# Average pooling over 512 MiB on one core: first loads moved ahead of the framework's closing barrier, sums as two additions, scaling on another engine

## The chip, the cores and the metric

The kernel runs on one core of one Trainium2 chip. The metric is the device time of one execution in microseconds (us): the median of several runs, lower is better.

Four of the core's engines appear here. VectorE (DVE in the profile) and ScalarE (ACT) do arithmetic, SyncE (SP) only issues transfers and passes semaphores, and GpSimd (POOL) sets a few constants at the start. Transfers between the chip's memory (HBM) and the on-chip buffer (SBUF, 128 partitions) are carried by 16 DMA engines; SyncE and ScalarE each have a queue through which they feed them.

## The reference

```python
x = randn(64, 256, 8192), float32;  kernel_size = stride = 4
for i in range(out_len):                       # 2048
    output[:, :, i] = np.mean(x[:, :, 4*i : 4*i + 4], axis=2)
```

Each output is the mean of four neighbouring inputs. 536.87 MB are read and 134.22 MB are written.

## The kernel before, in words

The input is taken as one flat array and cut into 64 blocks. A block is 128 partitions by 16,384 float32 (`FULL`), 8 MiB, and gives 128 by 4,096 means. Two input tiles, `xt[0]` and `xt[1]`, hold one block each; two output tiles, `ot[0]` and `ot[1]`, hold the means of two blocks each (a "pair").

The order on each engine is written by hand with semaphores. `take(engine, sem, n)` makes an engine wait until a semaphore is at least `n` and then lowers it by `n`. The framework's Tile context is closed at the start of the function (`tc.close()`, L36 in the profile), and everything after it is placed by hand.

- SyncE issues the loads. The first two go out ahead of the loop; later, `load(i, k)` goes out when VectorE has raised `free`, which says that `xt[k]` has been read. `full[k]` says that a load has landed.
- VectorE waits for `full[k]` (and, at a pair's first block, for `stored[q]`: the output tile's last store has landed). Then one `tensor_reduce` (L76) adds each group of four from `xt[k]` into half of `ot[q]`. After the second block of a pair, `scale` drains VectorE and multiplies the whole output tile by 1/4 (L67), raising `scaled`.
- ScalarE waits for `scaled` and issues the store of the pair (L87), 4 MiB.

`pair(i, q, ahead)` is one such round. The loop has 15 iterations of two pairs; one more pair follows, whose `ahead` issues the last two loads, the very last in three pieces (`TAIL`: 8192, 4608 and 3584 columns, each with a semaphore of its own). Blocks 62 and 63 are then done by `sums` (L92 to L94), which adds in two steps in place:

```python
nc.vector.tensor_tensor(out=t[:, : w // 2], in0=t[:, ::2], in1=t[:, 1::2], op=add)
nc.vector.drain()
nc.vector.tensor_tensor(out=o, in0=t[:, : w // 2 : 2], in1=t[:, 1 : w // 2 : 2], op=add)
```

Each result is scaled on VectorE and stored: block 62 from SyncE's queue (L127), the three pieces of block 63 from ScalarE's (L133).

Of the kernel before, what the change touches and what calls it, by code (L numbers as in the profile page):

```python
# [1 line left out]

# [4 lines left out]

FULL = 16384
PAIR = 2  # L10
ROUND = 2 * PAIR

TAIL = (8192, 4608, 3584)

@with_exitstack
def kernel(
    ctx: ExitStack,
    tc: tile.TileContext,
    x: bass.AP,  # L20
    kernel_size: bass.AP,
    stride: bass.AP,
    out: bass.AP,
):
    nc = tc.nc
    K, S = int(kernel_size), int(stride)
    assert K == S == 4
    B, C, L = x.shape
    assert L % K == 0
    P = nc.NUM_PARTITIONS  # L30
    dt = x.dtype
    add, mult = mybir.AluOpType.add, mybir.AluOpType.mult

    tc.close()
    tc.compile()  # L36

    M = FULL // K
    blocks = B * C * L // P // FULL
    loop = blocks - ROUND  # L40
    assert blocks * P * FULL == B * C * L and blocks % ROUND == 0 and sum(TAIL) == FULL
    xb = x.rearrange("b c l -> (b c l)").rearrange("(n p m) -> n p m", p=P, m=FULL)
    ob = out.rearrange("b c l -> (b c l)").rearrange("(n p m) -> p n m", p=P, m=M)

    xt0 = ctx.enter_context(nc.sbuf_tensor([P, FULL], dt))
    xt1 = ctx.enter_context(nc.sbuf_tensor([P, FULL], dt))
    ot0 = ctx.enter_context(nc.sbuf_tensor([P, PAIR * M], dt))
    ot1 = ctx.enter_context(nc.sbuf_tensor([P, PAIR * M], dt))
    xt, ot = [xt0, xt1], [ot0, ot1]

    full = [nc.alloc_semaphore(f"full{k}") for k in range(2)]
    piece = [nc.alloc_semaphore(f"piece{k}") for k in range(len(TAIL))]
    free = nc.alloc_semaphore("free")
    scaled = nc.alloc_semaphore("scaled")
    scaled_last = nc.alloc_semaphore("scaled_last")
    stored = [nc.alloc_semaphore(f"stored{k}") for k in range(2)]

    def take(engine, sem, n):
        engine.wait_ge(sem, n).then_inc(sem, -n)  # L60

    def load(i, k):
        nc.sync.dma_start(out=xt[k][:, :], in_=xb[i]).then_inc(full[k], 16)

    def scale(o, done):
        nc.vector.drain()  # L66
        means = nc.vector.tensor_scalar(out=o, in0=o, scalar1=1.0 / K, scalar2=None, op0=mult)  # L67
        means.then_inc(done, 1)

    def pair(i, q, ahead):  # L70

        for k in range(PAIR):
            take(nc.vector, full[k], 16)
            if k == 0:
                take(nc.vector, stored[q], 16)
            nc.vector.tensor_reduce(  # L76
                out=ot[q][:, k * M : (k + 1) * M],
                in_=xt[k][:, :].rearrange("p (m k) -> p m k", k=K),
                op=add,
                axis=mybir.AxisListType.X,  # L80
            ).then_inc(free, 1)
            take(nc.sync, free, 1)
            ahead(k)
        scale(ot[q][:, :], scaled)
        take(nc.scalar, scaled, 1)
        o = ot[q][:, :].rearrange("p (n m) -> p n m", n=PAIR)
        nc.scalar.dma_start(out=ob[:, bass.ds(i, PAIR), :], in_=o).then_inc(stored[q], 16)  # L87

    def sums(t, o, loaded):
        w = t.shape[1]  # L90
        take(nc.vector, loaded, 16)
        nc.vector.tensor_tensor(out=t[:, : w // 2], in0=t[:, ::2], in1=t[:, 1::2], op=add)  # L92
        nc.vector.drain()  # L93
        nc.vector.tensor_tensor(  # L94
            out=o, in0=t[:, : w // 2 : 2], in1=t[:, 1 : w // 2 : 2], op=add
        )

    for k in range(2):
        load(k, k)
        nc.scalar.sem_inc(stored[k], 16)  # L100

    edges = [sum(TAIL[:i]) for i in range(len(TAIL) + 1)]
    pieces = list(zip(edges[:-1], edges[1:]))
    xe, oe = xb[blocks - 1], ob[:, blocks - 1, :]

    def ahead_of_last(k):
        if k == 0:
            load(blocks - 2, 0)
        else:
            for sem, (a, b) in zip(piece, pieces):  # L110
                nc.sync.dma_start(out=xt[1][:, a:b], in_=xe[:, a:b]).then_inc(sem, 16)

    engines = (mybir.EngineType.SP, mybir.EngineType.DVE, mybir.EngineType.Activation)
    with nc.Fori(0, loop // ROUND, 1, engines=engines) as r:
        for q in range(2):
            i = r * ROUND + q * PAIR
            pair(i, q, lambda k: load(i + (PAIR + k), k))

    pair(loop, 0, ahead_of_last)

    take(nc.vector, stored[1], 16)
    o = ot[1][:, :M]
    sums(xt[0][:, :], o, full[0])
    scale(o, scaled_last)
    take(nc.sync, scaled_last, 1)
    nc.sync.dma_start(out=ob[:, blocks - 2, :], in_=o).then_inc(stored[1], 16)  # L127
    for sem, (a, b) in zip(piece, pieces):
        o = ot[1][:, M + a // K : M + b // K]
        sums(xt[1][:, a:b], o, sem)  # L130
        scale(o, scaled)
        take(nc.scalar, scaled, 1)
        nc.scalar.dma_start(out=oe[:, a // K : b // K], in_=o).then_inc(stored[1], 16)  # L133
    take(nc.sync, stored[0], 16)
    take(nc.sync, stored[1], 16 * (1 + len(TAIL)))

# [1 line left out]
_INS = ['x', 'kernel_size', 'stride']  # L139
_OUTS = [((64, 256, 2048), 'float32')]  # L140

_NUMBERS = {'kernel_size': 4, 'stride': 4}

# [26 lines left out]
```

## Time and profile before

| what | value |
|---|---|
| time, median of 3 runs | 1556.87 us (1556.68 to 1556.89) |
| the profiled execution: its own time | 1556.91 us |
| the profiled execution: its span | 1555.2 us |
| granted clock | 1.0 |
| VectorE busy | 1236.5 us, 80% of the span |
| ScalarE, TensorE arithmetic | none |
| bytes read and written | 536.87 MB and 134.22 MB, 432 GB/s over the span |

The span runs from the first to the last instruction; the time of the run is 1.7 us longer. The profile counts an engine as busy only while it does arithmetic; instructions that issue transfers, wait or raise semaphores are not counted. A group of instructions is shown by its line in the kernel, its engine, its operation, its tiles and shapes, and the mean duration of one in ns; behind the last bar stands the idle time of the engine ahead of them, and what ended it. In the tables of windows a DMA share of 1.00 means that all 16 DMA engines moved packets all the time; a packet is counted in the window in which it starts, so short windows can show more than 1.

### The profile page before, as it was taken

How to read it: one execution, taken by the hardware profiler on the slowest of the kernel's cores; microseconds unless marked ns; L12 is line 12 of the kernel's file. 1: busy time of each engine (PE TensorE's matmuls, PEld its weight loads, DVE VectorE, ACT ScalarE, POOL GpSimd, SP SyncE). 2: the span in 40 equal slices, each digit the busy share in tenths (PEclk: the TensorE clock that was granted, in tenths of full speed). 3: DMA queues.
4: the chain of work that ended last, by engine and by line, in shares of the span. 5: the costliest groups of instructions: out<-in, count | busy, mean ns of one | idle time of the engine just before them, and what ended most of it. 6: DMA issues, size and time to landing. Idle time of an engine off the chain costs nothing. (4 is left out here: it accounts for less than half of the span.)

```text
span 1555.2 us, 790 instructions
## 1 busy us (share of the span) xinstructions
DVE 1236.5 (80%) x105; POOL 0.2 (0%) x4
## 2 busy tenths in 40 slices
DVE  3968778787797877978779787797877977778778
POOL 0000000000000000000000000000000000000000
DMA  9999999999999999999999999999999999999999
GB/s 405 425 415 447 431 438 432 437 418 433 438 432 438 442 428 424 437 430 442 438 438 432 435 417 436 438 432 438 440 423 431 433 433 443 438 437 433 433 419 404
DMA packets 18512, 671.10 MB, mean 432 GB/s; under 512 B 1616, under 2 KB 1616, under 8 KB 1872
## 3 DMA queue, kind: packets, MB, share of 16 engines
q1 hardware_dynamic: 9648, 538.97, 80.1%
q10 hardware_dynamic: 8864, 132.12, 19.8%
HBM read 536.87 MB, written 134.22 MB: 432 GB/s over the span
## 5 line engine op out<-in xcount | busy, mean ns | idle before, releaser
L76 DVE TENSOR_REDUCE ot<-xt 128x4096 f32<-128x16384 f32 x62 | 1067.6, 17220 | 306.2 <-DVEq L60 306.2
L67 DVE TENSOR_SCALAR ot<-ot 128x8192 f32<-128x8192 f32 (+4 forms) x35 | 142.1, 4061 | 3.2
L92 DVE TENSOR_TENSOR xt<-xt 128x8192 f32<-128x8192 f32 (+3 forms) x4 | 17.7, 4424 | 4.1 <-DVEq L60 4.1
L94 DVE TENSOR_TENSOR ot<-xt 128x4096 f32<-128x4096 f32 (+3 forms) x4 | 9.2, 2292 | 0.3
L152 POOL MEMSET const-bfloat16-1.0<- 128x1 bf16 x1 | 0.1, 101 | 0.0
L152 POOL MEMSET const-uint8-127<- 128x1 uint8 x1 | 0.1, 101 | 0.0
L152 POOL MEMSET const-float32-0.0<- 128x1 f32 x1 | 0.1, 98 | 0.2 <-issue 0.2
L152 POOL MEMSET const-float32-1.0<- 128x1 f32 x1 | 0.1, 98 | 0.0
## 6 DMA issues: line engine op xcount, KB each, us to landing
out_dram<-ot ACTq DMA_DIRECT2D x31, 4096.0 KB, 50.4
xt<-in_x_dram SPq DMA_DIRECT2D x1, 4096.0 KB, 20.7
xt<-in_x_dram SPq DMA_DIRECT2D x1, 2304.0 KB, 31.2
out_dram<-ot SPq DMA_DIRECT2D x1, 2048.0 KB, 18.7
xt<-in_x_dram SPq DMA_DIRECT2D x1, 1792.0 KB, 35.6
out_dram<-ot ACTq DMA_DIRECT2D x1, 1024.0 KB, 11.8
xt<-in_x_dram SPq DMA_DIRECT2D x63, 30.7
out_dram<-ot ACTq DMA_DIRECT2D x1, 576.0 KB, 7.0
```

What stands on the lines that cost most here:

```text
L67: means = nc.vector.tensor_scalar(out=o, in0=o, scalar1=1.0 / K, scalar2=None, op0=mult)
L76: nc.vector.tensor_reduce(out=ot[q][:, k * M : (k + 1) * M], in_=xt[k][:, :].rearrange("p (m k) -> p m k", k=K), op=add, axis=mybir.AxisLi ...
L92: nc.vector.tensor_tensor(out=t[:, : w // 2], in0=t[:, ::2], in1=t[:, 1::2], op=add)
L94: nc.vector.tensor_tensor(out=o, in0=t[:, : w // 2 : 2], in1=t[:, 1 : w // 2 : 2], op=add)
L152: nc = _bacc.Bacc("TRN2", target_bir_lowering=False, num_devices=1)
```

## The change

1. The first two loads are issued ahead of `tc.close()` and `tc.compile()`. `load` returns its instruction, and the two names are put into `tc.no_tile_sem_insts`, so that Tile adds no semaphores of its own to them; they raise `full[0]` and `full[1]` as before.
2. In `pair`, `tensor_reduce` is replaced by `sums`: two additions in place with a drain between them. `sums` no longer waits itself; its callers do.
3. The pair is scaled on ScalarE (`nc.scalar.mul`) and no longer on VectorE. SyncE, which takes `free` after each block, raises the new semaphore `summed` after the second block of a pair and ahead of the load that it then issues; ScalarE takes `summed`, scales, raises `scaled`, takes it, and issues the store.
4. Ahead of the loop ScalarE multiplies a single column of zeros, so that its table (the activation function's data) is loaded there. It raises `stored[0]`.
5. In the tail, block 62 and the first two pieces of block 63 are scaled on ScalarE as well; the last piece (`b == FULL`) is still scaled on VectorE. The semaphore between VectorE and ScalarE is `summed_last`.

```diff
-    tc.close()
-    tc.compile()
...
     def load(i, k):
-        nc.sync.dma_start(out=xt[k][:, :], in_=xb[i]).then_inc(full[k], 16)
+        d = nc.sync.dma_start(out=xt[k][:, :], in_=xb[i])
+        d.then_inc(full[k], 16)
+        return d
...
+    for k in range(2):
+        tc.no_tile_sem_insts.add(load(k, k).ins.name)
+    tc.close()
+    tc.compile()
...
-            nc.vector.tensor_reduce(
-                out=ot[q][:, k * M : (k + 1) * M],
-                in_=xt[k][:, :].rearrange("p (m k) -> p m k", k=K),
-                op=add,
-                axis=mybir.AxisListType.X,
-            ).then_inc(free, 1)
+            sums(xt[k][:, :], ot[q][:, k * M : (k + 1) * M]).then_inc(free, 1)
             take(nc.sync, free, 1)
+            if k == 1:
+                nc.sync.sem_inc(summed, 1)
             ahead(k)
-        scale(ot[q][:, :], scaled)
+        take(nc.scalar, summed, 1)
+        nc.scalar.mul(ot[q][:, :], ot[q][:, :], 1.0 / K).then_inc(scaled, 1)
         take(nc.scalar, scaled, 1)
...
-    for k in range(2):
-        load(k, k)
-        nc.scalar.sem_inc(stored[k], 16)
+    zero = nc.const_aps.tensor(0.0, [P, 1], dt)
+    nc.scalar.mul(ot[0][:, :1], zero, 1.0).then_inc(stored[0], 16)
+    nc.scalar.sem_inc(stored[1], 16)
...
     take(nc.vector, stored[1], 16)
+    take(nc.vector, full[0], 16)
     o = ot[1][:, :M]
-    sums(xt[0][:, :], o, full[0])
-    scale(o, scaled_last)
+    sums(xt[0][:, :], o).then_inc(summed_last, 1)
+    take(nc.scalar, summed_last, 1)
+    nc.scalar.mul(o, o, 1.0 / K).then_inc(scaled_last, 1)
...
-        sums(xt[1][:, a:b], o, sem)
-        scale(o, scaled)
-        take(nc.scalar, scaled, 1)
+        take(nc.vector, sem, 16)
+        last = sums(xt[1][:, a:b], o)
+        if b == FULL:
+            nc.vector.drain()
+            last = nc.vector.tensor_scalar(
+                out=o, in0=o, scalar1=1.0 / K, scalar2=None, op0=mult
+            )
+        last.then_inc(summed_last, 1)
+        take(nc.scalar, summed_last, 1)
+        if b != FULL:
+            nc.scalar.mul(o, o, 1.0 / K).then_inc(scaled, 1)
+            take(nc.scalar, scaled, 1)
```

More of the change, by code (lines that the diff above doesn't have):

```diff
@@ L54 @@
     free = nc.alloc_semaphore("free")
+    summed = nc.alloc_semaphore("summed")
+    summed_last = nc.alloc_semaphore("summed_last")
     scaled = nc.alloc_semaphore("scaled")
@@ L62, in load, with sums @@
     def load(i, k):
-        nc.sync.dma_start(out=xt[k][:, :], in_=xb[i]).then_inc(full[k], 16)
-    def scale(o, done):
+        d = nc.sync.dma_start(out=xt[k][:, :], in_=xb[i])
[5 more added lines that the diff above has]
+    tc.compile()
+    def sums(t, o):
+        w = t.shape[1]
+        nc.vector.tensor_tensor(out=t[:, : w // 2], in0=t[:, ::2], in1=t[:, 1::2], op=add)
         nc.vector.drain()
-        means = nc.vector.tensor_scalar(out=o, in0=o, scalar1=1.0 / K, scalar2=None, op0=mult)
-        means.then_inc(done, 1)
+        return nc.vector.tensor_tensor(
+            out=o, in0=t[:, : w // 2 : 2], in1=t[:, 1 : w // 2 : 2], op=add
+        )
     def pair(i, q, ahead):
@@ L87, in pair @@
         nc.scalar.dma_start(out=ob[:, bass.ds(i, PAIR), :], in_=o).then_inc(stored[q], 16)
[L89 to L96, printed above, removed]
-    for k in range(2):
-        load(k, k)
-        nc.scalar.sem_inc(stored[k], 16)
+    zero = nc.const_aps.tensor(0.0, [P, 1], dt)
+    nc.scalar.mul(ot[0][:, :1], zero, 1.0).then_inc(stored[0], 16)
+    nc.scalar.sem_inc(stored[1], 16)
     edges = [sum(TAIL[:i]) for i in range(len(TAIL) + 1)]
@@ L129 @@
         o = ot[1][:, M + a // K : M + b // K]
-        sums(xt[1][:, a:b], o, sem)
-        scale(o, scaled)
-        take(nc.scalar, scaled, 1)
+        take(nc.vector, sem, 16)
[4 more added lines that the diff above has]
+                out=o, in0=o, scalar1=1.0 / K, scalar2=None, op0=mult
+            )
+        last.then_inc(summed_last, 1)
[3 more added lines that the diff above has]
+            take(nc.scalar, scaled, 1)
         nc.scalar.dma_start(out=oe[:, a // K : b // K], in_=o).then_inc(stored[1], 16)
```

## The prediction

> **What bounds the kernel now.** The page first: which resource has no slack.
>
> ```profile
> span 1555.2 us, 790 instructions
> DVE 1236.5 (80%) x105; POOL 0.2 (0%) x4
> q1 hardware_dynamic: 9648, 538.97, 80.1%
> q10 hardware_dynamic: 8864, 132.12, 19.8%
> ```
>
> VectorE works 80% of the span. The packets of the two DMA queues (q1: SyncE's loads, q10: ScalarE's stores) take 80.1 + 19.8 = 99.9% of all that 16 DMA engines have. The table of windows tells whether that is so everywhere.
>
> ```profile
> 0.00:2.40 2.40, 0.00 (x0) 0.20 (x4) 1.00 0.00 0
> 2.40:21.80 19.40, 0.00 (x0) 0.00 (x0) 1.00 1.03 432
> 21.80:41.20 19.40, 17.22 (x1) 0.00 (x0) 1.00 1.00 432
> 39.20:45.00 5.80, 3.79 (x2) 0.00 (x0) 1.00 0.92 362
> 44.04:48.88 4.84, 4.84 (x1) 0.00 (x0) 1.00 1.00 433
> 189.60:1399.20 1209.60, 972.35 (x76) 0.00 (x0) 1.00 1.00 434
> 1544.40:1550.40 6.00, 5.32 (x5) 0.00 (x0) 1.00 0.98 418
> 1550.40:1553.00 2.60, 0.00 (x0) 0.00 (x0) 1.00 0.97 399
> 1553.00:1555.20 2.20, 0.00 (x0) 0.00 (x0) 1.00 0.09 38
> ```
>
> Columns: window, its length, busy VectorE, busy GpSimd, granted clock, DMA share, GB/s. For 1,209.6 us in the middle the DMA share is 1.00 at 434 GB/s. There are three places where it is not full: the first 2.4 us; a dent near 42 us (5.8 us at 362 GB/s are 2.1 MB, which the row below it moves in 4.84 us: 1.0 us lost); and the last 2.2 us. The bytes are the same in both kernels, so only these places can give time, unless the change opens a new hole or slows the transfers. One round of the loop shows how far the loop is from a hole.
>
> ```profile
> 791.24 17.22 DVE L76 TENSOR_REDUCE ot<-xt 128x4096 f32<-128x16384 f32 x1 [2.66 <-DVEq L60]
> 815.20 17.22 DVE L76 TENSOR_REDUCE ot<-xt 128x4096 f32<-128x16384 f32 x1 [6.74 <-DVEq L60]
> 832.51 4.43 DVE L67 TENSOR_SCALAR ot<-ot 128x8192 f32<-128x8192 f32 x1
> 832.65 0.33 SPq L63 DMA_DIRECT2D xt<-in_x_dram  x1
> 837.18 0.38 ACTq L87 DMA_DIRECT2D out_dram<-ot  x1
> 839.60 17.22 DVE L76 TENSOR_REDUCE ot<-xt 128x4096 f32<-128x16384 f32 x1 [2.66 <-DVEq L60]
> ...
> out_dram<-ot ACTq DMA_DIRECT2D x31, 4096.0 KB, 50.4
> ```
>
> A pair of blocks takes 839.60 - 791.24 = 48.36 us. VectorE idles before each reduction, for data. The load that refills a tile goes out at 832.65, while the other tile's load lands near 839.5: 6.9 us in which the next load already waits behind the running one. The loop stays DMA bound as long as this lead is over the time from a load's issue to its first data: at the start, issue at 1.39 (row below) and nothing before 2.4, so 1.0 us.
>
> **Part 1: VectorE's sums in the loop.** The reduction becomes two additions with a drain, and the scaling leaves VectorE. All shapes stand in the old tail:
>
> ```profile
> L76 DVE TENSOR_REDUCE ot<-xt 128x4096 f32<-128x16384 f32 x62 | 1067.6, 17220 | 306.2 <-DVEq L60 306.2
> L67 DVE TENSOR_SCALAR ot<-ot 128x8192 f32<-128x8192 f32 x31 | 137.2, 4427 | 2.9
> L92 DVE TENSOR_TENSOR xt<-xt 128x8192 f32<-128x8192 f32 x1 | 8.7, 8693 | 2.6 <-DVEq L60 2.6
> L94 DVE TENSOR_TENSOR ot<-xt 128x4096 f32<-128x4096 f32 x1 | 4.4, 4425 | 0.1
> ```
>
> 8.69 + 0.08 + 4.43 = 13.2 us instead of 17.22 per block, 4.0 less; with the scaling gone VectorE has 26.4 us of work per pair, not 38.9. All of it is cover: loads go out 4.0 us earlier, the lead grows from 6.9 to about 10.9 us, and the DMA engines are as full as before. Worth in the loop: 0. If the lead were lost instead, each missing us would be paid 31 times.
>
> **Part 2: scaling on ScalarE.** No ScalarE arithmetic stands in this trace. From below: VectorE's scaling of the same tile, 4.43 us. From above: the reduction, 17.22, the longest single instruction. I take 8.7, the addition that also writes 8,192 elements: it lies between the two, and is the more cautious of the two rows of that size. In the round shown, the sums would end at 815.20 + 13.2 = 828.4 and the store go out at 828.4 + 8.7 + 0.1 = 837.2, where it goes out now (837.18). It must be home before the same output tile is used again at 839.60 + 48.36 = 887.96; it takes 50.4 us, so 837.6 is the latest issue that delays nothing, and ScalarE may take 9.1 us. Later than that VectorE would wait, still without a hole: the sum that frees a tile may start 10.9 - 1.0 = 9.9 us late before the DMA engines run dry. Worth: 0 up to some 19 us of ScalarE time.
>
> The Trainium skill, page "ScalarE: Activation LUTs", section "Rules for kernel authors", speaks against this part: multiplications belong on VectorE, not on ScalarE. The section "What ACT_TABLE_LOAD costs" of the same page prices an activation with immediate scale at 186 ns plus 0.833 ns per element, by which I estimate 7.0 us here; the store would go out at 835.5, the sum would be the same, and VectorE's 4.43 us is indeed less than either.
>
> The table's load stands ahead of the loop on ScalarE, where nothing is queued but the first scaling, due after both first blocks have landed and been summed (42.62 + 13.2 = 55.8 us). Cover: all of that; cost 0. If it ran in front of the first store anyway, that store would still meet a full DMA. On SyncE one semaphore increment is added in front of every second load, a queue step below 0.1 us, covered by the lead.
>
> **Part 3: the first two loads, and the dent.** Rows:
>
> ```profile
> SPq L152 <- PEq L152: 0.5, 1, 0.5
> SPq L36 <- PEq L36: 0.5, 2, 0.3
> ...
> 1.39 0.87 SPq L63 DMA_DIRECT2D xt<-in_x_dram  x2
> ...
> 23.40 17.22 DVE L76 TENSOR_REDUCE ot<-xt 128x4096 f32<-128x16384 f32 x1 [23.40 <-DVEq L60]
> 40.90 19.52 SPq L63 DMA_DIRECT2D xt<-in_x_dram  x2
> 42.62 17.22 DVE L76 TENSOR_REDUCE ot<-xt 128x4096 f32<-128x16384 f32 x1 [2.01 <-DVEq L60]
> ```
>
> SyncE passes the program's opening barrier (L152), then two barriers of the closing Tile context (L36), then issues the loads at 1.39. Now they stand in front of `tc.close()`: the L152 wait stays, the two L36 waits (0.5 us) come after them. At least 0.5; at most 1.39 - 0.5 = 0.9; I take 0.6, the two waits and the instructions between them. The other engines pass those barriers later by the 0.87 us of the two issues; VectorE is not needed until 23 us, so that is covered.
>
> The dent: the third load goes out only after the first reduction, at 40.90, and its data start at about 41.9, when the second load has just been drained. With the new sums it goes out 4.0 us earlier, about 5 us ahead of that point. The 1.0 us goes. Bounds 0 (if the restart is lost at another place) and 1.1.
>
> **Part 4: the tail.** Rows:
>
> ```profile
> 1516.53 8.69 DVE L92 TENSOR_TENSOR xt<-xt 128x8192 f32<-128x8192 f32 x1 [2.61 <-DVEq L60]
> 1532.01 4.42 DVE L92 TENSOR_TENSOR xt<-xt 128x4096 f32<-128x4096 f32 x1
> 1532.18 0.34 SPq L127 DMA_DIRECT2D out_dram<-ot  x1
> 1541.21 2.56 DVE L92 TENSOR_TENSOR xt<-xt 128x2304 f32<-128x2304 f32 x1 [1.11 <-DVEq L60]
> 1545.29 0.76 DVE L67 TENSOR_SCALAR ot<-ot 128x1152 f32<-128x1152 f32 x1
> 1546.44 2.03 DVE L92 TENSOR_TENSOR xt<-xt 128x1792 f32<-128x1792 f32 x1 [0.39 <-DVEq L60]
> 1549.71 0.63 DVE L67 TENSOR_SCALAR ot<-ot 128x896 f32<-128x896 f32 x1
> ...
> out_dram<-ot ACTq DMA_DIRECT2D x1, 448.0 KB, 4.7
> ```
>
> The last chain: the last piece lands (1546.4), sum, drain, scaling to 1550.3, store, 4.7 us to landing. It keeps its instructions, since the last piece is still scaled on VectorE. The stores ahead of it move: block 62's sum ends at 1516.53 + 13.2 = 1529.7 and ScalarE, at the addition's 8.69 us / 8,192 = 1.06 ns per element, needs 4.3 us for 4,096, so its store goes out at 1534.1 instead of 1532.18; piece 1's sum ends at 1545.2 and ScalarE's 1.2 us for 1,152 put its store 0.5 us later than now. Both meet DMA engines that are full until 1553 (0.98 and 0.97 above), so their bytes are only reordered; ScalarE is free by 1547, ahead of the last store. I take 0, with -0.7 (loads overtake stores, and a third of the last 2.2 us is filled) to +1.0 (the late 2 MB store is still draining when the last one comes; the 2.2 us at 0.09 leave room for about this).
>
> **Sum.** The profiled run took 1556.91 us, 1.7 over its span and 0.04 over the median 1556.87, so no correction is due. -0.6 (loads) -1.0 (dent) + 0 (loop) + 0 (tail) = -1.6: **1555.3 us**.
>
> **Rivals.** *A: the loads do not get ahead, or the start is paid back.* The early loads only move the idle time, because the end hangs on the last store: nothing to gain but the tail's shift, 1556 to 1558. Against it: with share 1.00 throughout, a us won at the start has nowhere to be lost. It lies within 0.2% too.
>
> *B (slower): closing the Tile context waits for the two loads that are in flight.* Then VectorE starts when the second load has landed, at 42.6 instead of 23.4; the first tile is free 13.2 us later, at 55.8, new data come at 56.8, and the DMA engines stand idle for 56.8 - 42 = 15 us: 1556.9 - 0.6 + 15 - 1 = about 1570. It decides as soon as the barrier ends later than 42 - 13.2 - 1.0 = 28 us. For it: no drain with loads in flight precedes a barrier in this trace. Against: the loads carry semaphores of the kernel's own, on which only VectorE waits. Chance 0.03.
>
> *C (slower): more SBUF traffic slows the transfers.* VectorE now also writes and rereads the half sums, and ScalarE reads and writes beside it. A rate of 432 instead of 434 GB/s would cost 7 us: 1562. Against: 432 GB/s with VectorE idle (2.40 to 21.80) and with it busy (21.80 to 41.20). The Trainium skill, page "SBUF — State Buffer", section "SBUF: two separate sides", goes further: a DMA cannot be slowed by an engine's access at all; the trace agrees for the reduction, and no run here shows ScalarE beside it. Chance 0.04, with ScalarE over 19 us another 0.01 (at 20 us the store cycle would lose half a us per pair, 15 in all).
>
> *D (faster than forecast):* 0.9 + 1.1 + 0.7 are 2.7 us, so over 0.2% asks for more: all of the last 2.2 us filled as well, 1552 to 1553.7. For it only the 0.09 in the last row. Chance 0.04.
>
> **How the numbers follow.** 0.2% of 1556.87, about what a measurement of this kernel can tell from no change, is 3.1 us: faster is below 1553.8, slower above 1560.0. The forecast has 0.76 and rival A 0.12, together 0.88 for "same"; D 0.04; B and C 0.08 for slower. The range: 1556.9 - 2.7 = 1554.2 below, and above A's middle, 1557.2; this leaves out D, B, C and part of A.
>
> **What would show it.** The profile after should have the first load near 0.75 us, windows around 42 us at 433 GB/s, the third load's issue near 36 us, ScalarE at 7 to 9 us per pair, VectorE near 55% busy, DMA share 1.00 in the middle, and a pair every 48.36 us. A pair period over 48.4, a first VectorE addition after 28 us, or a DMA share below 1.00 in the loop would make the prediction wrong.

## The result and the profile after

The changed kernel takes 1553.59 us (median of 16 runs, 1553.3 to 1555.7) against 1556.72 us before (16 runs, 1556.5 to 1557.05): ratio 0.9981, 95% interval 0.9974 to 0.9989. That is 3.1 us less, twice the forecast 1.6, and 0.6 us below the range. Of the 16 runs 13 lie at 1553.3 to 1553.7 and three at 1555.2 to 1555.7; the profiled one is one of these three (1555.70 us, span 1554.0). A second profile is of a run at 1553.43 us (span 1551.7); below, "the 1555.70 run" and "the 1553.43 run" are these two.

The page of the 1555.70 run: the same saturated DMA engines, VectorE with 54% instead of 80%, ScalarE with 15%.

```profile
span 1554.0 us, 946 instructions
DVE 840.8 (54%) x133; ACT 226.1 (15%) x36; POOL 0.2 (0%) x4
q1 hardware_dynamic: 9648, 538.97, 80.1%
q10 hardware_dynamic: 8864, 132.12, 19.8%
```

Four of its groups by line and shape (count | busy us, mean ns | idle before):

```profile
L75 DVE TENSOR_TENSOR xt<-xt 128x8192 f32<-128x8192 f32 x63 | 547.6, 8692 | 697.4 <-DVEq L59 697.4
L77 DVE TENSOR_TENSOR ot<-xt 128x4096 f32<-128x4096 f32 x63 | 278.8, 4426 | 4.7
L93 ACT ACTIVATE ot<-ot 128x8192 f32<-128x8192 f32 x31 | 217.9, 7029 | 1289.6 <-ACTq L59 1289.6
L100 ACT ACT_TABLE_LOAD x1 | 1.3, 1283 | 2.4 <-PEq L71 2.4
```

The additions cost in the loop what they cost in the old tail (8.69 and 4.43 us). ScalarE scales a pair in 7.03 us; I had taken 8.7, and the Trainium skill's page "ScalarE: Activation LUTs", section "What ACT_TABLE_LOAD costs", gave the estimate of 7.0, with which the trace agrees.

The timeline of the 1555.70 run (start, us, engine, line), from the first load to the loop; only the lines used here are shown, and a line with x2 or x4 stands for several issues and spans them:

```profile
0.74 55.42 SPq L62 DMA_DIRECT2D xt<-in_x_dram  x4
23.09 8.69 DVE L75 TENSOR_TENSOR xt<-xt 128x8192 f32<-128x8192 f32 x1 [23.09 <-DVEq L59]
36.58 19.58 SPq L62 DMA_DIRECT2D xt<-in_x_dram  x2
42.30 8.69 DVE L75 TENSOR_TENSOR xt<-xt 128x8192 f32<-128x8192 f32 x1 [6.01 <-DVEq L59]
61.76 8.69 DVE L75 TENSOR_TENSOR xt<-xt 128x8192 f32<-128x8192 f32 x1 [6.25 <-DVEq L59]
87.03 8.69 DVE L75 TENSOR_TENSOR xt<-xt 128x8192 f32<-128x8192 f32 x1 [12.09 <-DVEq L59]
114.80 8.69 DVE L75 TENSOR_TENSOR xt<-xt 128x8192 f32<-128x8192 f32 x1 [14.58 <-DVEq L59]
...
790.05 8.69 DVE L75 TENSOR_TENSOR xt<-xt 128x8192 f32<-128x8192 f32 x1 [11.22 <-DVEq L59]
834.69 0.38 ACTq L96 DMA_DIRECT2D out_dram<-ot  x1
838.40 8.69 DVE L75 TENSOR_TENSOR xt<-xt 128x8192 f32<-128x8192 f32 x1 [11.21 <-DVEq L59]
```

The first load goes out at 0.74 (before: 1.39), the third at 36.58 (40.90), and a pair takes 838.40 - 790.05 = 48.35 us, as before. The same view of the 1553.43 run:

```profile
61.68 8.69 DVE L75 TENSOR_TENSOR xt<-xt 128x8192 f32<-128x8192 f32 x1 [6.51 <-DVEq L59]
85.18 8.69 DVE L75 TENSOR_TENSOR xt<-xt 128x8192 f32<-128x8192 f32 x1 [10.31 <-DVEq L59]
112.92 8.69 DVE L75 TENSOR_TENSOR xt<-xt 128x8192 f32<-128x8192 f32 x1 [14.55 <-DVEq L59]
...
787.77 8.69 DVE L75 TENSOR_TENSOR xt<-xt 128x8192 f32<-128x8192 f32 x1 [11.20 <-DVEq L59]
836.13 8.69 DVE L75 TENSOR_TENSOR xt<-xt 128x8192 f32<-128x8192 f32 x1 [11.19 <-DVEq L59]
```

The two runs are together at the third block (61.76 and 61.68) and 1.85 us apart at the fourth (87.03 and 85.18). They stay apart, 2.3 us in the loop, to the end, with the same 48.36 us per pair. The gap opens between the third and the fourth block, the time in which the first store, issued near 63 us, begins. What it is shows at the end of the run, in the windows of the 1555.70 run (length, busy VectorE, ScalarE, GpSimd, clock, DMA share, GB/s):

```profile
39.20:44.04 4.84, 1.74 (x1) 0.00 (x0) 0.00 (x0) 1.00 1.00 433
...
189.60:1399.20 1209.60, 656.57 (x101) 175.73 (x25) 0.00 (x0) 1.00 1.00 433
...
1550.50:1551.30 0.80, 0.00 (x0) 0.00 (x0) 0.00 (x0) 1.00 1.01 412
1551.30:1552.00 0.70, 0.00 (x0) 0.00 (x0) 0.00 (x0) 1.00 0.33 129
1552.00:1553.00 1.00, 0.00 (x0) 0.00 (x0) 0.00 (x0) 1.00 0.06 24
1553.00:1554.00 1.00, 0.00 (x0) 0.00 (x0) 0.00 (x0) 1.00 0.04 14
```

and of the 1553.43 run:

```profile
1549.50:1550.50 1.00, 0.00 (x0) 0.00 (x0) 0.00 (x0) 1.00 1.02 417
1550.50:1551.30 0.80, 0.00 (x0) 0.00 (x0) 0.00 (x0) 1.00 0.60 242
1551.30:1552.00 0.70, 0.00 (x0) 0.00 (x0) 0.00 (x0) 1.00 0.00 0
```

The dent near 42 us is gone (share 1.00 at 433 GB/s). In the 1555.70 run the DMA share falls to 0.06 between 1552 and 1553: one of 16 engines (1/16 = 0.0625) still has work. In the 1553.43 run all 16 stop within 0.4 us of each other. The table of landings says the same for the whole run. The trace marks each transfer's landing 16 times, read here as once for each DMA engine; each column is the last mark less the eighth, in us, in the one profiled run of each kernel whose time stands beside its name (for the last store, the last 16 marks of a semaphore that four stores share):

```
kernel (its profiled run)          third load  fourth load  block 62  last store
before (1556.91)                         0.45         1.64      1.96        1.70
after, run at 1555.70                    0.58         2.08      2.63        2.02
after, run at 1553.43                    0.28         0.32      0.33        0.27
early loads alone (1555.92)              1.75         2.20      1.75        1.50
sums alone (1554.20)                     0.25         0.40      0.73        0.73
additions in first round (1554.49)       0.37         0.38      0.35        0.90
reduction in first round (1556.54)       1.95         2.50      2.32        1.53
hole of about 2 us (1557.00)             0.59         2.05      1.82        1.33
hole of about 5 us (1560.60)             0.37         2.16      2.58        2.06
```

Before, one engine trails the eighth by 1.6 to 2.0 us from the fourth load to the last store (the fifteenth by 1.1 to 1.5), and the kernel ends when that engine ends: its last landing is at 1555.17, SyncE's last instruction at 1555.18. In all five profiled runs with a hole near 42 us an engine is at least 1.6 us behind at the fourth load; of the nine without one, only in the run at 1555.70. At the third load, the first behind the hole, it shows in two of the five only (1.75 and 1.95). So the runs tie the trailing engine to the hole, but do not show that the hole itself sets it back.

### The profile page after: what moved, and what is told of

Its sections match the earlier page's. It is cut to its first block, busy times and chain, and to the rows that moved or that the text cites. A ratio compares the mean times of both kernels' runs of the same rounds, so it can differ in the third digit from the quotient of the medians.

```text
span 1554.0 us, 946 instructions
## 1 busy us (share of the span) xinstructions
DVE 840.8 (54%) x133; ACT 226.1 (15%) x36; POOL 0.2 (0%) x4
## 5 line engine op out<-in xcount | busy, mean ns | idle before, releaser
L75 DVE TENSOR_TENSOR xt<-xt 128x8192 f32<-128x8192 f32 (+1 forms) x66 | 556.6, 8434 | 703.6 <-DVEq L59 703.6
L93 ACT ACTIVATE ot<-ot 128x8192 f32<-128x8192 f32 x31 | 217.9, 7029 | 1289.6 <-ACTq L59 1289.6
L77 DVE TENSOR_TENSOR ot<-xt 128x4096 f32<-128x4096 f32 (+1 forms) x66 | 283.6, 4296 | 4.9
L128 ACT ACTIVATE ot<-ot 128x4096 f32<-128x4096 f32 x1 | 3.6, 3617 | 17.2 <-ACTq L59 17.2
```

The lines of the kernel that those rows point to most:

```text
L77: return nc.vector.tensor_tensor(out=o, in0=t[:, : w // 2 : 2], in1=t[:, 1 : w // 2 : 2], op=add)
L93: nc.scalar.mul(ot[q][:, :], ot[q][:, :], 1.0 / K).then_inc(scaled, 1)
L128: nc.scalar.mul(o, o, 1.0 / K).then_inc(scaled_last, 1)
```

## The experiments

Theory after the result: the part of the gain that the forecast missed belongs to the hole near 42 us, which costs more than its length because it leaves an engine behind. Rivals: the loop itself has become faster; the early loads or ScalarE's scaling brought the rest. Each time is a median of 11 runs; the kernel before stands at 1556.73 to 1556.75 (33 runs beside each set of four).

**Early loads alone.** The kernel before with

```diff
+    for k in range(2):
+        tc.no_tile_sem_insts.add(load(k, k).ins.name)
     tc.close()
     tc.compile()
```

> The kernel before, with its first two loads issued ahead of the closing of the Tile context and nothing else changed. Forecast's theory (each hole in the DMA engines is worth its own length): first load at 0.74 instead of 1.39, dent near 42 us still there, so 1556.7 - 0.65 = 1556.1 us. Rival (the start decides how far one of the 16 DMA engines falls behind the others, and the whole extra gain comes from there): the last landing of a load trails the other 15 by under 0.5 us instead of 1.5 and the time is 1554.5 to 1555.

Measured 1556.12 us (1555.59 to 1556.49), ratio 0.9996 (0.9987 to 1.0005): 0.61 less, as forecast; the interval alone would not tell it from nothing, but two more pairs of kernels below give 0.6 as well. The hole is still there, and two engines trail (the table above):

```profile
0.74 59.26 SPq L61 DMA_DIRECT2D xt<-in_x_dram  x4
...
40.47 19.53 SPq L61 DMA_DIRECT2D xt<-in_x_dram  x2
42.20 17.22 DVE L81 TENSOR_REDUCE ot<-xt 128x4096 f32<-128x16384 f32 x1 [2.01 <-DVEq L58]
```

**Sums alone.** The kernel before with

```diff
-            nc.vector.tensor_reduce(out=ot[q][...], in_=xt[k]..., op=add, axis=...).then_inc(free, 1)
+            nc.vector.tensor_tensor(out=t[:, : FULL // 2], in0=t[:, ::2], in1=t[:, 1::2], op=add)
+            nc.vector.drain()
+            nc.vector.tensor_tensor(out=o, in0=t[:, : FULL // 2 : 2], in1=t[:, 1 : FULL // 2 : 2], op=add).then_inc(free, 1)
```

> The kernel before, with the reduction replaced by two additions with a drain, scaling still on VectorE and the loads still late. Forecast's theory: the third load goes out near 36.9 instead of 40.9, the dent goes, 1.0 us: 1555.7. Rival (the dent is also what puts one DMA engine behind the others): 1.0 + 1.1 to 1.9 us: 1553.8 to 1554.6, with the landings of all 16 engines within 0.6 us.

Measured 1554.19 us (1553.94 to 1554.41), ratio 0.9983 (0.9974 to 0.9992): 2.5 us less, where the forecast has 1.0. The missing 1.5 us is in this part of the change (0.4 us of it lies outside the span, see below).

**The changed kernel with late loads.** Its two loads stand behind `tc.close()` again.

> The changed kernel, with its first two loads issued after the closing of the Tile context, as before. Forecast's theory: 0.65 us above the changed kernel's usual 1553.5: 1554.2. If scaling on ScalarE is worth nothing it equals the kernel with the sums alone. Rival (early loads carry the extra gain): 1555.7 or more.

Measured 1554.19 us (1553.94 to 1556.12): 0.6 over the changed kernel, and equal to the sums alone.

**The changed kernel again.**

> The changed kernel once more, for a second profile. 13 of 16 runs took 1553.3 to 1553.7, three 1555.2 to 1555.7, among them the profiled one, in which one of the 16 DMA engines lands its share of each load 2.3 us after the other 15. Theory of the trailing engine: a run at 1553.5 shows all 16 within 0.6 us in the loop, and the same 48.36 us per pair. Rival (the loop is faster in the quick runs): a pair takes 48.30 us and the spread stays at 2.3 us.

Measured 1553.60 us (1553.28 to 1555.45; two of 11 near 1555.3). The profile at 1553.43 shown above is of this set: same pair time, no trailing engine. A faster loop is ruled out.

**Sums and early loads, scaling on VectorE.** The changed kernel without points 3 to 5 of the change.

> The kernel before with early loads and the two additions, scaling still on VectorE: the changed kernel without its third part. If the holes at the start add up, 1554.2 (sums alone) - 0.6 (early loads) = 1553.6 us, the changed kernel's usual time, so ScalarE's part is worth nothing. If ScalarE's earlier store is what sometimes puts one DMA engine behind (7 of 38 runs of kernels that scale on ScalarE lay 2 us higher, 0 of 11 with the sums alone), no run here lies near 1555.5; if early loads do it, one or two of 11 do.

Measured 1553.61 us (1553.40 to 1555.19), equal to the changed kernel: ScalarE's part is worth nothing. One run of the 11 lies near 1555.5 (1555.19; another at 1554.61), and three kernels below that scale on VectorE and load late have such runs too (two or three of 11 each), so neither ScalarE's scaling nor the early loads are needed for them.

This zero is a sum, however. The time of a run less its span is 1.7 us in the kernel before, in the one with early loads alone and in those that scale on ScalarE; it is 1.3 us in the eight, most of them below, that use the additions in the loop or ahead of it and scale on VectorE. By the median spans the sums alone gain 2.1 us (1555.0 to 1552.9) and 0.4 outside the span; and ScalarE's part makes the span 0.4 us shorter (1552.3 to 1551.9) and the rest 0.4 us longer. Only those eight traces have a packet of 8,192 bytes of the queue named `instruction` in their last 22 us. Whether that is the reason no run shows.

**Which blocks matter.** A round of four blocks is taken out of the loop; in one kernel it alone uses the additions, in the mirror it alone uses the reduction.

```diff
+    for q in range(2):
+        pair(q * PAIR, q, lambda k: load(q * PAIR + PAIR + k, k), first=True)
-    with nc.Fori(0, loop // ROUND, 1, engines=engines) as r:
+    with nc.Fori(1, loop // ROUND, 1, engines=engines) as r:
...
+            if first:                # the mirror: if not first
+                ...                  # two additions
+            else:
+                ...                  # tensor_reduce
```

> The kernel before, with the two additions in the first four blocks alone (a round of two pairs taken out of the loop) and the reduction in the other 58. Theory (the whole gain of the sums is the hole near 42 us, 1.0 us of its own and 1.5 us because it leaves one DMA engine behind the others for the rest of the run): 1554.2, as with the sums everywhere. Rival (the longer lead of the loads in the loop lets the trailing engine catch up): 1555.7, the hole's own 1.0 us.

Measured 1554.40 us (1554.23 to 1555.98). Its third load:

```profile
36.90 19.52 SPq L63 DMA_DIRECT2D xt<-in_x_dram  x2
```

> The mirror: the reduction in the first four blocks, the two additions in the other 58. Theory (the hole alone): 1556.7, the time before, with one engine's landings 1.5 us behind until the end. Rival (the longer lead in the loop): 1555.2 to 1555.7, the engine catching up within the loop.

Measured 1556.71 us (1556.08 to 1556.96), ratio 0.9999 (0.9990 to 1.0008). Its third load:

```profile
41.03 19.51 SPq L63 DMA_DIRECT2D xt<-in_x_dram  x2
```

The two kernels differ in the first four blocks alone and have the same 1.3 us outside the span: these four blocks hold 2.3 us, and the longer lead of the loads in the other blocks is worth nothing in the time (the span is 0.4 us longer than before, 1555.4 against 1555.0, and the rest 0.4 us shorter). No engine catches up in the loop (1.95 us behind at the third load, 2.32 at block 62).

**How the price depends on the hole.** VectorE clears an unused tile in front of the signal that frees the first input tile, which puts the third load off:

```diff
+            if first and q == 0 and k == 0:
+                last = nc.vector.memset(ot[1][:, :N], 0.0)
             last.then_inc(free, 1)
```

> As the kernel with the reduction in the first four blocks, with a memset of 4,096 columns on VectorE in front of the signal that frees the first tile, so that the third load goes out 2 to 4.4 us (X) later and the hole near 42 us is X longer. Theory (what an engine falls behind comes from the restart, not from the hole's length): 1556.7 + X, spread between the engines as before. Rival (the lag grows with the hole): 1556.7 + X + at least 1 us, and the spread grows with it.

> As the kernel with the longer hole, with a memset of 1,024 columns: the third load goes out near 42.7, the hole is about 2.7 us (1.0 with the reduction alone, 5.1 with 4,096 columns, which took 1559.6, just 5.2 us over the kernel without a hole). Theory (a short hole costs 1.5 us beyond its length because the engines run dry one by one, some before and some after the new packets reach them; a long one costs its length, since all are empty by then): 1554.4 + 2.7 = 1557.1 with the landings of the third load within 0.6 us. Rival (every hole costs 1.5 us more than its length, and the long one was luck): 1558.6.

> The two additions in the first four blocks, with a memset of 3,072 columns in front of the first free: the third load goes out near 40.3 and its data are due near 41.3, while the second load's last packets are still under way, so there is next to no hole. Theory (what counts is that the engines run dry at different times): some engines run dry and some do not, 1555 to 1556 us, spread of the third load over 0.6 us. Rival (the loss is the hole's length, times about 2.5): 1554.4 to 1554.8.

> As the last one, with 2,048 columns: the third load goes out near 39.4, its data are due 1.5 us before the second load ends. Both theories: no engine runs dry, 1554.4 us, as with the additions alone in the first round; more than 1555 would mean that a lead of 1.5 us over the first-data time is not enough, and the rule for a lead must be larger.

The first two have the reduction in the first round, the last two the additions. Where the third load went out, by the timelines, and the times:

| kernel | third load issued, us | time, us (11 runs) |
|---|---|---|
| additions in the first round | 36.90 | 1554.40 |
| additions, memset of 2,048 | 38.92 | 1554.35 (1554.10 to 1555.84) |
| additions, memset of 3,072 | 39.93 | 1554.49 (1554.11 to 1556.08) |
| reduction in the first round | 41.03 | 1556.71 |
| reduction, memset of 1,024 | 42.27 | 1556.76 (1556.28 to 1557.51) |
| reduction, memset of 4,096 | 45.12 | 1559.60 (1559.33 to 1561.28) |

The last two, from the timelines of the kernel with 1,024 columns

```profile
41.26 0.91 DVE L96 MEMSET ot<- 128x1024 f32 x1 [0.16 <-issue]
42.27 18.71 SPq L63 DMA_DIRECT2D xt<-in_x_dram  x2
```

and of that with 4,096:

```profile
41.55 3.47 DVE L96 MEMSET ot<- 128x4096 f32 x1 [0.80 <-issue]
45.12 17.40 SPq L63 DMA_DIRECT2D xt<-in_x_dram  x2
```

This is a step. Up to 39.93 the issue's moment costs nothing; between 39.93 and 41.03 it costs 2.2 us at once; from 41.03 to 42.27 nothing more; and from there to 45.12, 2.85 us later, 2.84 us. By the eighth landing of the third load (61.66 with the additions, 62.79, 63.84 and 66.59 with the reduction) the three holes are 1.1, 2.2 and 4.9 us long; they cost 2.3, 2.4 and 5.2 us against 1554.40. So the theory as I put it for the first of these kernels (1556.7 + X, here 1556.7 + 4.1 = 1560.8) is wrong for most of its runs, the rival with it; the theory for the second (1.5 us beyond its length for a short hole, nothing beyond it for a long one) comes near in the time, but not in its reason: behind both longer holes an engine is 2.0 to 2.2 us behind at the fourth load all the same. The third kernel's theory expected some engines to run dry at 39.93; they did not, 1554.49 is the rival's time.

What a hole is paid for can be read from the packets in the traces. Their lengths are summed over both queues and divided by 16, and each profiled run is compared with that of the additions in the first round (1554.49), in us per engine:

| profiled run | span | idle, 41 to 48 us | packets take longer by | idle after 1500 us |
|---|---|---|---|---|
| reduction in the first round (1556.54) | +2.05 | +0.61 | +0.88 | +0.69 |
| reduction, memset of 1,024 (1557.00) | +2.51 | +1.27 | +0.82 | +0.30 |
| reduction, memset of 4,096 (1560.60, 1.0 above its median) | +6.11 | +4.27 | +0.89 | +1.07 |

The engines' idle time is the smaller part of the short hole. The 16 packets right behind a hole take 3.05 to 3.17 us on average instead of 2.42, which is 0.64 to 0.75 of the 0.8 to 0.9 us; the last column is idle time at the end, in which the others wait for the engine that ends last. From 48 to 1500 us the idle time is the same within 0.02 us, so the other loads of the first round leave no hole of their own. No kernel here has the hole with the additions in the first four blocks.

**A warmed queue.** The changed kernel with one load of 128 rows of 64 bytes on ScalarE's queue at the start:

```diff
+    nc.scalar.dma_start(out=ot[1][:, :16], in_=xb[0][:, :16]).then_inc(warm, 16)
+    take(nc.vector, warm, 16)
```

> The changed kernel, with one small load (128 rows of 64 bytes into an unused tile) issued on ScalarE's queue at the start, so that the first store at 63 us is not the queue's first use. Theory (the packets of 2.5 to 3.2 us instead of 2.418 between 65 and 85 us come from the queue's first use, and they set one engine behind in the runs near 1555.5): about 0.5 to 0.8 us less, 1552.8 to 1553.1, and no run near 1555.5. Rival (they come from the first writes meeting loads, whatever the queue did before): 1553.6, with the same slow runs.

Measured 1553.65 us (1553.36 to 1555.83; four of 11 between 1554.7 and 1555.8): the rival. The small load landed only 22.7 us after its issue, so the first addition starts at 25.55 and the third load goes out at 39.04, which by the table above costs nothing. In its profile 49 packets that start between 58 and 90 us take over 2.5 us (45 and 18 in the two runs of the changed kernel), and no engine trails. The queue's first use is not what makes the beginning of the first store uneven, and longer packets there do not by themselves set an engine back.

## Why the prediction was right or wrong

- **The bound** was right: a DMA share of 1.00 before and after, at 434 and 433 GB/s. A third of VectorE's busy time (1236.5 to 840.8 us) went without moving the loop.
- **Part 1, the loop: 0.** Right. The pair takes 48.36 us in both; in all blocks but the first four the reduction costs nothing in the time (1556.71 with the additions there, 1556.75 without).
- **Part 2, ScalarE: 0.** Right in the time (1553.61 without it, 1553.60 with it), in part by luck: 0.4 us less in the span and 0.4 us more outside it, of which the prediction says nothing. 7.03 us instead of the 8.7 that I took, and the limit of 9.1 us was not reached. The rule against such scaling of the Trainium skill, page "ScalarE: Activation LUTs", section "Rules for kernel authors", holds for the duration, 7.03 against 4.43 us, but not for this time, since the work is hidden.
- **Part 3, the first loads: -0.6.** Right: 0.61 alone, 0.59 between the changed kernel with late and with early loads, 0.58 with the sums on VectorE.
- **Part 3, the dent: -1.0, bounds 0 and 1.1.** This is the step that failed, in its size: a hole was priced at its own length. The dent is worth 2.3 us in the pair of kernels that differ in the first round only (2.5 with the sums alone, 0.4 of it outside the span). Its length was read rightly: the third load lands 1.1 us later with it. That 1.1 holds the 0.6 us of idle time and about half of the 0.9 us by which packets take longer in that pair; the other half and the wait for the engine that ends last, 0.7 us, the prediction left out. I read the cost off windows near 42 us, which show a mean over 16 engines; the share of one engine hardly moves that mean: an engine 2 us behind is 2/16 = 0.1 us there. The row with the hint stood in the prediction: 1553.00 to 1555.20 at a share of 0.09, in which I saw nothing but room for the last stores, is by the landings mostly one or two engines that end late (the eighth engine's last store lands at 1553.5, the last at 1555.2). With the additions in the first round, where no engine trails in the loop, the last is 0.9 us behind the eighth there, not 1.7.
- **Part 4, the tail: 0.** Right in the time: 0.6 + 2.5 = 3.1 us account for the whole result. In the spans it is 0.6 + 2.1 + 0.4, and the last 0.4 comes with scaling on ScalarE, for the most part after 1500 us (the DMA engines idle 0.78 us there without it, 0.35 with it); it is lost again outside the span.
- **Rivals.** A: the start was not paid back. B: the first addition starts at 23.09, so the barrier does not wait for loads in flight. C: 433 GB/s with VectorE at 54% and ScalarE beside it (Trainium skill, page "SBUF — State Buffer", section "SBUF: two separate sides": the trace agrees). D asked for the last 2.2 us to be filled as well and gave 1552 to 1553.7: time and sign came true in the runs near 1553.5, where all engines end together. It named no cause, and the experiments find it near 42 us, not in the tail.

What stays open: why packets take longer behind a hole, why in runs with a hole one engine (in three of the profiles two) falls about 2 us behind, and why in some runs without a hole (5 of 27 of the changed kernel by their times; the one profiled shows it) an engine falls as far behind about when the first store begins. No kernel here beats the changed one; the one with additions, early loads and scaling on VectorE equals it.

## What to carry to other kernels

Where the DMA engines are full throughout, look for the places where the next load goes out just as the last one ends, at the start above all: here one load issued 1.1 us later cost 2.2 us for the whole run, and shorter VectorE work in 58 other blocks gave nothing. Price such a hole by more than its idle time, and by the engine that ends last, not by the mean share of 16: here a tail of windows at 0.06 to 0.1 meant that one or two engines carried the rest. Before moving work to another engine, ask whether the path to the end sees it: ScalarE's scaling and 396 us less of VectorE work are worth nothing here.

## What the runs showed of the hardware

- One DMA engine can stay about 2 us behind the others through a saturated loop: in the 1555.70 run it lands 1.9 us behind the fifteenth at the fourth load (87 us) and 2.35 at block 62 (1515 us). In no profile does the lag to the eighth change by more than 0.6 us between these two.
- Three DMA holes near 42 us, with 0.6, 1.3 and 4.3 us of idle time, cost 2.3, 2.4 and 5.2 us.
- From 190 us on no packet of 65,536 bytes takes over 2.45 us in any profile, and nearly all take 2.418. The first 16 of a run take 2.9 to 3.2 us on average, and so do the first 16 behind a hole; while the first store starts beside the loads single ones take up to 3.4 us, and a small earlier transfer on the same queue did not change that.
- SyncE got past the closing barriers with two loads in flight: the first addition starts at 23.09, at the first load's landing, and not at the second's (42.17).
